# Strassen steps that split their raw blocks first, five raw slots, transfers on ScalarE's queue: one composite edit of a hybrid decoder block

## The chip, the cores and the metric

The kernel runs on one core of a Trainium2 chip. The metric is the device time of one execution in microseconds (us); lower is better. A profiled execution gives the page and the trace from which every duration below is read.

## The reference, cut to what matters

One decoder block on 256 tokens of width 4096, all in float32:

```python
h = rmsnorm(x, norm_w)                       # 256 x 4096
proj = h @ w_in                              # 4096 x 20480
u_p, z_p, u_c, b_c, c_c, z_c, g_logit = split(proj)   # 2048 each, g_logit 8192
y_pool = (pooled_means(u_p) @ pool_w) * pool_scale * silu(z_p)
y_conv = b_c * (conv3(c_c * u_c) + conv_b) * silu(z_c)
br = [y_pool @ w_branch[0], y_conv @ w_branch[1]]     # 2048 x 4096 each
merged = sum(sigmoid(g_logit + gate_b) * br)
out = rmsnorm(x + merged @ w_out, final_norm_w)
```

Nearly all work is in the three products with `w_in`, `w_branch` and `w_out`. Every weight is used once, so all weights stream through the core.

## The kernel before, in words

**Units and steps.** The products are cut into 32 units of 1024 output columns: 20 for `w_in` (names `cz`, `cb`, `cu`, `cc` for the convolution branch, `pz`, `pu` for the pooling branch, `g` for the gates), 8 for `w_branch` (`b`) and 4 for `w_out` (`o`). A unit is a row of steps; a step multiplies 256 tokens by one 256 x 1024 block of weights. A `w_in` or `w_out` unit has 16 steps, a `w_branch` unit 8. Each float32 value is split in two parts, a rounded high part and the rest, and each product is made of three matmuls (high by high, high by low, low by high).

**Two kinds of steps.** A plain step, `P`, is eight block products: 24 matmuls of 128 x 512. A Strassen step, `S`, is seven block products: 21 matmuls, paid for with sums of weight blocks that are formed on the core (and with sums of activations that stand ready in `arena`). The texts such as `NINE` or `TEN` give the order of P and S steps of a unit; `NINE` has nine S, `TEN` ten, `SIX5` six.

**What a step needs.** The weight block of 128 x 2048 is loaded into one of `NRAW = 4` slots of `raw` (`issue_load`, line 993) by SP's queue. For an S step the load is cut in two, and a third, accumulating DMA by POOL's queue adds quarter 2 into quarter 3. Then the block is prepared: ScalarE rounds high parts into cells of `ring` (`highs`, line 245), VectorE subtracts to get low parts (`lows`, line 249). In an S step of before, ScalarE rounds all four quarters, VectorE forms three sums in `parts` (function `added`, line 305), and `split` (line 312) makes high and low parts of the sums. A P step holds 8 cells of the ring of `CELLS = 27`, an S step 14; TensorE's groups free them two by two.

**What sets the order.** The program order of every engine is written out by hand. `pump` (line 1009) issues loads, the next one as soon as the step `NRAW` before it is prepared in program order, and lays preparation as far ahead as the ring has cells. Work after a unit (its epilogue) is a queue of items, one taken for every six matmuls; `gap(n)` is n empty items. `combine` (line 442) evacuates the Strassen corner sums `J` into the result: for late units by two accumulating DMAs by POOL's queue (`gather`). All plain transfers between buffers and DRAM scratch (`move`, line 82: gates, merged rows, stage fills, row parameters) go to SP's queue, in program order among the weight loads. `evacuate` (line 421) copies a finished PSUM bank to `E` or `Y`, and a new unit's first matmul into this bank comes after it.

A unit with ten S steps holds one more activation operand than stands in the arena; it is swapped into `side` by a DMA of POOL's queue (`side_load`, line 544), once in such a unit.

Of the kernel before, what the change touches and what calls it, by code (L numbers as in the profile page):

```python
# [15 lines left out]
P = 128  # L16
T = 256
D = 4096
HALF = D // 2
# [4 lines left out]
KB = 256  # L24

ND, NS, NB = 8, 6, 2
CELLS = 27
NRAW = 4
EARLY = 3
AHEAD = 4  # L30
TICK = 6
# [6 lines left out]
SEVEN3 = "PPPSPSPSPSPSPSPS"  # L38
NINE = "PSPSPSPSSPSPSSPS"
NINE_A = "PSPSSPSPSSPSPSPS"  # L40
NINE_P = "PSPSSPSPSSPSSPSP"
HOST = "PPBPPMMPSSPSSPSSPSS"
TEN = "PSPSSPSSPSSPSSPS"
OUT3 = "PSPSPSPSPSPSSPPP"
# [7 lines left out]
def hybrid_block(ctx: ExitStack, tc: tile.TileContext, x, xc, prm, rows_in, w_in, pool_w, w_branch, w_out, out):  # L52
# [27 lines left out]
        return pin(nc.scalar.dma_start(dst, src))  # L80

    def move(dst, src):
        return pin(nc.sync.dma_start(dst, src))

    def aside(dst, src):
        return pin(nc.gpsimd.dma_start(dst, src))
# [10 lines left out]
    def sb(name, shape, dt=F32):  # L97
        return upper.tile(shape, dt, name=name)
# [8 lines left out]
    J = blocks("J", [P, 4, NH])  # L107
    ident = blocks("ident", [P, P])
    raw = sb("raw", [P, NRAW, 2 * NU])
    parts = sb("parts", [P, 3, NH])  # L110
    sa = sb("sa", [P, 8, P])
    Y = sb("Y", [P, 2, NU])
    par = sb("par", [P, 112])
# [131 lines left out]
    def highs(cells, src):  # L245
        for i, c in runs(cells):
            act(ring[:, c], src[:, i])
# [11 lines left out]
    class Step:  # L259
# [7 lines left out]
        def first(self):  # L267
            if self.kind == "B":
                return []

            def rounded(cells):
                self.q = self.raw.rearrange("p (i c) -> p i c", i=4)
                self.cells = cells
                if self in steps[:2]:
                    for i in range(4):
                        if self is steps[0] and i == 0:
                            copy(ring[:, cells[0]], self.q[:, 0])
                        else:
                            highs(cells[i:i + 1], self.q[:, i:i + 1])
                elif self.halved:  # L280
                    for i in (0, 2):
                        highs(cells[i:i + 2], self.q[:, i:i + 2])
                else:
                    highs(cells, self.q)

            return [(4, None, rounded)]

        def rest(self):
            if self.kind == "P":
                def rests(to):  # L290
                    self.lows = to
                    if self in steps[:2]:
                        for i in range(4):
                            if self is steps[0] and i % 2 == 0:
                                x_low(0, 1 - i // 2)
                            lows(to[i:i + 1], self.cells[i:i + 1], self.q[:, i:i + 1])
                    elif self.halved:
                        for i in (0, 2):
                            lows(to[i:i + 2], self.cells[i:i + 2], self.q[:, i:i + 2])
                    else:  # L300
                        lows(to, self.cells, self.q)

                return [(4, None, rests)] + self.mid
            if self.kind == "S":
                def added(to):
                    q, d = self.q, self.cells
                    self.lows = to
                    sub(parts[:, 0], q[:, 3], q[:, 1])
                    lows(to[3:4], d[3:4], q[:, 3:4])
                    sub(parts[:, 1:3], q[:, 0:3:2], parts[:, 0:1].to_broadcast([P, 2, NH]))  # L310

                def split(cells):
                    self.sum_cells, self.sum_lows = cells[0:3], cells[3:6]
                    highs(cells[0:1], parts[:, 0:1])
                    highs(cells[1:3], parts[:, 1:3])
                    lows(self.lows[0:3], self.cells[0:3], self.q[:, 0:3])
                    lows(cells[3:6], cells[0:3], parts)

                return [(4, None, added)] + self.mid + [(6, None, split)]
            if self.kind == "B":  # L320
                def base(cells):
                    self.cells, self.lows = cells[0:4], cells[4:8]
                    highs(self.cells, quarters(E))
                    lows(self.lows, self.cells, quarters(E))

                return [(8, lambda: self.unit.flags.get("base"), base)]

            def pooled(cells):
                self.pool_cells, self.pool_lows = cells[0:2], cells[2:4]
                q = quarters(E)[:, 2 * self.g:2 * self.g + 2]  # L330
                highs(self.pool_cells, q)
                lows(self.pool_lows, self.pool_cells, q)

            def rests(to):
                self.lows = to
                lows(to, self.cells, self.q)

            return [(4, None, rests), (4, lambda: self.unit.flags.get(f"pooled{self.g}"), pooled)]
# [2 lines left out]
            return cell(self.cells[i]), cell(self.lows[i]), [self.cells[i], self.lows[i]]  # L341

        def formed(self, i):
            return cell(self.sum_cells[i]), cell(self.sum_lows[i]), [self.sum_cells[i], self.sum_lows[i]]

        def groups(self):
            gs = []
# [18 lines left out]
            else:  # L366
# [1 line left out]
                prods = {"M1": (A11, plain(2), ("F", 0, 0)),  # L368
                         "N3": (Q3, plain(1), ("E", 0, 0)),
                         "M2": (A12, plain(0), ("E", 0, 1)),  # L370
                         "N5": (Q5, plain(3), ("F", 0, 1)),
                         "N6": (Q6, formed(0), ("F", 1, 1)),
                         "N4": (A22, formed(1), ("E", 1, 1)),
                         "N7": (Q7, formed(2), ("F", 1, 0))}
# [67 lines left out]
    def combine(u):  # L442
        d = u.dst
        if u.s:
            corner_sums(u)
            assert u.cornered
            q = J.rearrange("p (n t) c -> p t n c", n=2)
            d4 = d.rearrange("p t (n c) -> p t n c", n=2)
            if u.late:
                for t, n in ((0, 4), (1, 2)):  # L450
                    queue.extend(gap(n) + [lambda t=t: gather(d4[:, t], q[:, t])])
            elif u.scaled:
                for t in range(2):
                    stt(d4[:, t], q[:, t], rin[:, t:t + 1], d4[:, t], ALU.mult, ALU.add)
            else:
                add(d4, d4, q)
        u.flags["base"] = True
        hush[0] = now[0] + (HUSH if u.late else 0)
        quiet[0] = now[0] + QUIET
        if u.urgent:  # L460
            u.urgent()
# [96 lines left out]
    def silu_y(late):  # L558
        def silu(t):
            act(Y[:, t], Y[:, t], AF.Silu, **(dict(scale=rin[:, t:t + 1]) if late else {}))  # L560
        return gap(12 if late else 3) + [lambda: silu(0), None, lambda: silu(1)]

    def rescale(d):
        return gap(12) + [lambda: act(d[:, 0], d[:, 0], scale=rin[:, 0:1]), None,
                          lambda: act(d[:, 1], d[:, 1], scale=rin[:, 1:2])]

    def conv_units(c, first):
        base = 2 * HALF + c * NU

        def b_epi(u):  # L570
            def product(t):
                stt(E[:, t], E[:, t], rin[:, t:t + 1], Y[:, t], ALU.mult, ALU.mult)
            return gap(12) + [lambda: product(0), None, lambda: product(1)] + gap(5) + [lambda: move(g_d[c], E)]

        def c_epi(u):
            def inner(j):
# [16 lines left out]
                        kb = 8 * c + b  # L593
                        stt(y[:, b, s:], v[:, i, 0:T - s], tap_col(2 - s, kb), y[:, b, s:], ALU.mult, ALU.add)

            items = [lambda: move(Y, g_d[c])] + gap(6) + pairs(transposes(E, inner)) + gap(5) + pairs(transposes(Y, outer))
            for j, n in enumerate((1, 7, 8, 8)):
                items += gap(n) + [lambda j=j: taps(j)]
            return items + [None, lambda: mul(chan(E), chan(J), chan(Y))] + gap(5) + [lambda: put(y_d[1, c], chan(E))]

        u = in_unit(f"cz{c}", base + 3 * HALF, lambda u: silu_y(u.late) + (gap(4) + side_items(ND - 1) + side_items(ND - 2) if first else []),
                    FIRST if first else SIX5, dst=Y)
        u.late = not first
        in_unit(f"cb{c}", base + HALF, b_epi, TEN if c else NINE_A).late = True
        u = in_unit(f"cu{c}", base, lambda u: rescale(Y), NINE, dst=Y)
        u.late = True
        in_unit(f"cc{c}", base + 2 * HALF, c_epi, NINE_A).urgent = lambda: mul(E, E, Y)

    def pool_units(c):
        u = in_unit(f"pz{c}", HALF + c * NU, lambda u: silu_y(True) + gap(4) + band_items(c), HOST if c else SIX5, dst=Y)  # L610
        u.late = True
        in_unit(f"pu{c}", c * NU, lambda u: [], NINE_P).urgent = lambda: None

    def band_items(c):
        if c == 0:
# [114 lines left out]
    def branch_unit(n, c):  # L730
        def epi(u):
# [16 lines left out]
            def stored():  # L748
                put(m_d[c], chan(turned))
                merged[c] = now[0] + STORED  # L750
            return gap(2) + [gated, None, lambda: add(E, E, Y), None,
                lambda: c < 3 and move(Y, gates_d[0, c + 1])] + gap(4) + pairs(transposes(E, copy)) + gap(4) + [stored]

        text = (B1 if c else B1_FIRST) if n else B0_MORE if c else B0
        u = Unit(f"b{n}_{c}", lambda i: w_branch[n, c, i], seq_y(text), y_ops[n], epi)
# [7 lines left out]
    def out_unit(c):  # L763
# [5 lines left out]
        def epi(u):  # L769
            def row(t):  # L770
                gather(E[:, t], xrows[:, t, cs])

            def square(t):
                act(Y[:, 1], E[:, t], AF.Square, accum_out=ossq[:, t, c:c + 1])
            return gap(8) + [lambda: row(0), None, None, lambda: row(1)] + gap(12) + [start] + gap(6) + [
                lambda: square(0), lambda: square(1),
                lambda: mul(E, E, Y[:, 0:1].to_broadcast([P, 2, NU]))] + gap(5) + [lambda: move(o_d[c], E)]

# [341 lines left out]
    for u in units:  # L1120
# [28 lines left out]
        for st in u.steps:  # L1149
            assert st.prepared, (u.name, st.kind)  # L1150
            run_step(u, st)
            if u.text is TEN and st.kind == "S" and st.op in x_ops[:ND] and st is not u.steps[-1]:
                side_load(2 * ND - 3 - x_ops.index(st.op))
            state["now"] += 1
            if state["now"] == OPENED:
# [114 lines left out]
```

## Time and profile before

| what | value |
|---|---|
| median of 3 runs | 2411.51 us (2397.87 to 2412.62) |
| the profiled execution | 2411.59 us |
| its span, first to last instruction | 2409.9 us |
| TensorE (PE) busy | 2356.2 us, 98% |
| VectorE (DVE) busy | 2085.2 us, 87% |
| ScalarE (ACT) busy | 1499.1 us, 62% |
| mean HBM rate | 251 GB/s |

Times in the profile are counted from the first instruction. PE is TensorE's matmuls, PEld its weight loads, DVE is VectorE, ACT ScalarE, POOL GpSimd, SP SyncE. Consecutive matmuls overlap in the records, so a busy PE is not one at its peak; how many matmuls start in a stretch says more. A wait is shown with the engine, tile and line that ended it.

### The profile page before, as it was taken

The page shows a single profiled execution, that of the slowest core. Times are in us where ns is not written, and L with a number is a line of the kernel's source. Part 1 is how long each engine was busy: PE and PEld are TensorE (multiplying, and loading weights), DVE is VectorE, ACT ScalarE, POOL GpSimd, SP SyncE. Part 2 cuts the span into 40 slices and gives each one's busy share as a digit, 9 for nine tenths or more (in the row PEclk, how much of TensorE's full clock was granted, in tenths as well). Part 3 has the DMA queues.
Part 4 walks back from the last instruction along what each step waited for, and adds up shares of the span by engine and source line. Part 5 has one row for each costly group of instructions (what it writes and reads, how often), then busy time and mean ns, then how long its engine had stood idle before and what let it go on. Part 6 is the DMA issues. An engine that isn't in the chain of part 4 may idle for free.

```text
span 2409.9 us, 28848 instructions
## 1 busy us (share of the span) xinstructions
PE 2356.2 (98%) x10424; PEld 1938.3 (80%) x10424; DVE 2085.2 (87%) x2034; ACT 1499.1 (62%) x1590; POOL 284.8 (12%) x342
## 2 busy tenths in 40 slices
PE   9999999999999999999999999999999999999996
PEld 7888888888888788788787787778888888887875
DVE  8789888998889879879898898888898889898967
ACT  6665656666666556656666666666666656566654
POOL 0011100110101101101111111111000000011110
PEclk9999999999999999999999999999999999999998
DMA  9789876988868768768998899899878788888986
GB/s 369 233 262 273 242 261 204 280 264 247 262 224 243 236 206 246 249 207 247 282 276 265 257 294 270 254 301 270 285 243 288 254 279 287 258 239 276 289 261 237
DMA packets 167712, 627.71 MB, mean 260 GB/s; under 512 B 17424, under 2 KB 25872, under 8 KB 135568
## 3 DMA queue, kind: packets, MB, share of 16 engines
q1 hardware_dynamic: 118864, 526.04, 61.1%
q0 software_dynamic: 48128, 98.59, 23.1%
q8 instruction: 81, 1.33, 0.2%
q10 hardware_dynamic: 576, 1.24, 0.1%
q14 instruction: 63, 0.52, 0.1%
HBM read 579.66 MB, written 25.17 MB: 251 GB/s over the span
## 4 chain that ended last, share of the span: by engine, by line
PE 73%; DMA 14%; DVE 8%; issue 3%; ACT 2%; POOL 0%; SPq 0%; DVEq 0%; ACTq 0%; POOLq 0%
PE sums L1048 54%; PE shared L1048 17%; DMA raw<-in_w_in_dram 9%; DVE ring L62 5%; DMA gates_d<-E 2%; DMA raw<-in_w_out_dram 2%; DVE parts L62 2%; ACT ring L59 1%; PE shared L693 1%; DMA E<-J 1%; PE shared L479 1%; DMA Y<-in_rows_dram 1%; DMA o_d<-E 0%; ACT E L59 0%; DVE J L62 0%
## 5 line engine op out<-in xcount | busy, mean ns | idle before, releaser
L1048 PE MATMUL sums<-ring,arena 128*128 128x512 f32 x7011 | 1653.3, 391 | 37.4 <-DVE ring L62 22.2
L1048 PEld LDWEIGHTS sums<-ring,arena 128*128 128x128 f32 x7011 | 1314.7, 188 | 324.7 <-DVE ring L62 31.8
L62 DVE TENSOR_TENSOR ring<-raw,ring 128x512 fp32r<-128x512 f32 (+3 forms) x904 | 1085.6, 1220 | 148.2 <-ACT ring L59 77.5
L59 ACT ACTIVATE ring<-raw 128x1024 fp32r<-128x1024 f32 (+3 forms) x661 | 882.8, 1370 | 323.7 <-DMA raw<-in_w_in_dram 101.3
L59 ACT ACTIVATE ring<-parts 128x1024 fp32r<-128x1024 f32 (+1 forms) x451 | 372.6, 840 | 384.8 <-DVE parts L62 290.1
L1048 PE MATMUL shared<-ring,arena 128*128 128x512 f32 x2241 | 542.0, 389 | 0.1
L1048 PEld LDWEIGHTS shared<-ring,arena 128*128 128x128 f32 x2241 | 421.0, 188 | 88.4 <-DVE ring L62 0.5
L62 DVE TENSOR_TENSOR ring<-parts,ring 128x1536 fp32r<-128x1536 f32 (+2 forms) x258 | 391.6, 1529 | 29.8 <-ACT ring L59 19.5
L89 POOL DMA_DIRECT2D raw<-in_w_in_dram x168 | 145.4, 866 | 1408.3 <-DMA raw<-in_w_in_dram 559.5
L62 DVE TENSOR_TENSOR parts<-raw,parts 128x1024 f32<-128x1024 f32 x222 | 270.6, 1219 | 0.0
L62 DVE TENSOR_TENSOR parts<-raw 128x512 f32<-128x512 f32 x222 | 152.4, 687 | 37.9 <-issue 31.1
L62 DVE TENSOR_TENSOR J<-J 128x512 f32<-128x512 f32 (+1 forms) x90 | 78.3, 870 | 39.3 <-ACT J L59 36.8
L1048 PE MATMUL sums<-ring,last_pair 128*128 128x512 f32 x306 | 77.1, 390 | 3.6 <-DVE ring L62 3.6
L59 ACT ACTIVATE E<-sums 128x512 f32<-128x512 f32 x76 | 42.0, 598 | 54.9 <-DMA gates_d<-E 25.9
L59 ACT ACTIVATE J<-shared 128x512 f32<-128x512 f32 x128 | 68.7, 626 | 11.7 <-PE shared L479 10.7
L1048 PEld LDWEIGHTS sums<-ring,last_pair 128*128 128x128 f32 x306 | 57.2, 188 | 16.6 <-DVE ring L62 4.9
L89 POOL DMA_DIRECT2D raw<-in_w_out_dram x31 | 27.1, 873 | 287.1 <-DMA raw<-in_w_out_dram 180.9
L89 POOL DMA_DIRECT2D raw<-in_w_branch_dram x23 | 20.0, 869 | 298.3 <-DMA raw<-in_w_branch_dram 174.3
L1048 PE MATMUL shared<-ring,last_pair 128*128 128x512 f32 x216 | 51.9, 389 | 0.0
L1048 PE MATMUL shared<-ring,side 128*128 128x512 f32 x207 | 50.7, 389 | 0.0
L1048 PEld LDWEIGHTS shared<-ring,last_pair 128*128 128x128 f32 x216 | 40.5, 188 | 8.5
L1048 PEld LDWEIGHTS shared<-ring,side 128*128 128x128 f32 x207 | 38.9, 188 | 8.1
(124 smaller groups left out, 674.5 us busy)
## 6 DMA issues: line engine op xcount, KB each, us to landing
raw<-in_w_in_dram SPq DMA_DIRECT2D x150, 1024.0 KB, 7.0
raw<-in_w_in_dram SPq DMA_DIRECT2D x168, 768.0 KB, 6.4
raw<-in_w_in_dram SPq DMA_DIRECT2D x176, 256.0 KB, 5.5
raw<-in_w_in_dram POOLq DMA_DIRECT2D x168, 256.0 KB, 6.7
raw<-in_w_branch_dram SPq DMA_DIRECT2D x41, 1024.0 KB, 7.4
raw<-in_w_out_dram SPq DMA_DIRECT2D x33, 1024.0 KB, 7.2
raw<-in_w_out_dram SPq DMA_DIRECT2D x31, 768.0 KB, 6.8
raw<-in_w_branch_dram SPq DMA_DIRECT2D x23, 768.0 KB, 6.3
```

Of the source, the lines that this page charges most:

```text
L59: return pin(nc.scalar.activation(dst, src, func, **kw))
L62: return pin(nc.vector.tensor_tensor(out=dst, in0=a, in1=b, op=op))
L89: return pin(nc.gpsimd.dma_start(dst, src, accum_op=ALU.add))
L479: pin(nc.tensor.transpose(shared(j)[:, i * T + t * P:i * T + (t + 1) * P], src[:, t, c:c + P], ident))
L693: pin(nc.tensor.matmul(o, a, b, start=(k, i) == (0, 0), stop=(k, i) == (3, 2)))
L1048: pin(nc.tensor.matmul(ps, lhs, rhs, start=n == 0, stop=n == u.total[b] - 1))
```

## The change

An S step keeps the same sums, written to other places. ScalarE first rounds the three plain quarters that are used as they are (0, 1, 2) and VectorE makes their low parts (`whole`). Then VectorE writes the sums over the raw block itself (quarter 1 becomes quarter 3 minus quarter 1, then quarters 0 and 2 have it subtracted), and the four formed quarters are split in two pairs (`outer`, `inner`). `parts` is gone, `raw` has five slots, the ring 26 cells. `move` goes to ScalarE's queue. `cz1`, `cu0`, `cu1`, `cc0`, `cc1`, `pz0`, `pu0`, `pu1` have one S step in place of a P step each. Gaps in several epilogues are shifted by one to six items.

```diff
-CELLS = 27
-NRAW = 4
+CELLS = 26
+NRAW = 5
...
-NINE_P = "PSPSSPSPSSPSSPSP"
+TEN_P = "PSPSSPSSPSSPSSSP"
+SEVEN5 = "PPPPPSPSPSSPSPSS"
...
     def move(dst, src):
-        return pin(nc.sync.dma_start(dst, src))
+        return pin(nc.scalar.dma_start(dst, src))
...
-    parts = sb("parts", [P, 3, NH])
...
-                    highs(cells, self.q)
-            return [(4, None, rounded)]
+                    highs(cells, self.q[:, 0:len(cells)])
+            return [(3 if self.kind == "S" else 4, None, rounded)]
...
-                def added(to):
-                    q, d = self.q, self.cells
+                def whole(to):
                     self.lows = to
-                    sub(parts[:, 0], q[:, 3], q[:, 1])
-                    lows(to[3:4], d[3:4], q[:, 3:4])
-                    sub(parts[:, 1:3], q[:, 0:3:2], parts[:, 0:1].to_broadcast([P, 2, NH]))
-                def split(cells):
-                    self.sum_cells, self.sum_lows = cells[0:3], cells[3:6]
-                    highs(cells[0:1], parts[:, 0:1])
-                    highs(cells[1:3], parts[:, 1:3])
-                    lows(self.lows[0:3], self.cells[0:3], self.q[:, 0:3])
-                    lows(cells[3:6], cells[0:3], parts)
-                return [(4, None, added)] + self.mid + [(6, None, split)]
+                    lows(to, self.cells, self.q[:, 0:3])
+                def outer(cells):
+                    q = self.q
+                    self.outer = cells
+                    sub(q[:, 1], q[:, 3], q[:, 1])
+                    sub(q[:, 0:3:2], q[:, 0:3:2], q[:, 1:2].to_broadcast([P, 2, NH]))
+                    highs(cells[0:2], q[:, 1:4:2])
+                    lows(cells[2:4], cells[0:2], q[:, 1:4:2])
+                def inner(cells):
+                    q = self.q
+                    self.inner = cells
+                    highs(cells[0:2], q[:, 0:3:2])
+                    lows(cells[2:4], cells[0:2], q[:, 0:3:2])
+                return [(3, None, whole)] + self.mid + [(4, None, outer), (4, None, inner)]
...
-                         "N5": (Q5, plain(3), ("F", 0, 1)),
+                         "N5": (Q5, formed(3), ("F", 0, 1)),
...
             if u.late:
-                for t, n in ((0, 4), (1, 2)):
+                for t, n in ((0, 2), (1, 1)):
                     queue.extend(gap(n) + [lambda t=t: gather(d4[:, t], q[:, t])])
...
-        return gap(12 if late else 3) + [lambda: silu(0), None, lambda: silu(1)]
+        return gap(15 if late else 3) + [lambda: silu(0), None, lambda: silu(1)]
     def rescale(d):
-        return gap(12) + [lambda: act(d[:, 0], d[:, 0], scale=rin[:, 0:1]), None,
+        return gap(14) + [lambda: act(d[:, 0], d[:, 0], scale=rin[:, 0:1]), None,
...
-                    FIRST if first else SIX5, dst=Y)
+                    FIRST if first else SEVEN5, dst=Y)
...
-        u = in_unit(f"cu{c}", base, lambda u: rescale(Y), NINE, dst=Y)
+        u = in_unit(f"cu{c}", base, lambda u: rescale(Y), TEN, dst=Y)
...
-        in_unit(f"cc{c}", base + 2 * HALF, c_epi, NINE_A).urgent = lambda: mul(E, E, Y)
+        in_unit(f"cc{c}", base + 2 * HALF, c_epi, TEN).urgent = lambda: mul(E, E, Y)
...
-        u = in_unit(f"pz{c}", HALF + c * NU, lambda u: silu_y(True) + gap(4) + band_items(c), HOST if c else SIX5, dst=Y)
+        u = in_unit(f"pz{c}", HALF + c * NU, lambda u: silu_y(True) + gap(4) + band_items(c), HOST if c else SEVEN5, dst=Y)
...
-        in_unit(f"pu{c}", c * NU, lambda u: [], NINE_P).urgent = lambda: None
+        in_unit(f"pu{c}", c * NU, lambda u: [], TEN_P).urgent = lambda: None
...
-            return gap(8) + [lambda: row(0), None, None, lambda: row(1)] + gap(12) + [start] + gap(6) + [
+            return gap(6) + [lambda: row(0), None, lambda: row(1)] + gap(12) + [start] + gap(8) + [
...
-            if u.text is TEN and st.kind == "S" and st.op in x_ops[:ND] and st is not u.steps[-1]:
+            if u.text in (TEN, TEN_P) and st is next(q for q in u.main if q.kind == "S"):
                 side_load(2 * ND - 3 - x_ops.index(st.op))
```

More of the change, by code (lines that the diff above doesn't have):

```diff
@@ L343, in formed @@
         def formed(self, i):
-            return cell(self.sum_cells[i]), cell(self.sum_lows[i]), [self.sum_cells[i], self.sum_lows[i]]
+            c, j = ((self.outer, 0), (self.inner, 0), (self.inner, 1), (self.outer, 1))[i]
+            return cell(c[j]), cell(c[2 + j]), [c[j], c[2 + j]]
         def groups(self):
@@ L572, in product @@
                 stt(E[:, t], E[:, t], rin[:, t:t + 1], Y[:, t], ALU.mult, ALU.mult)
-            return gap(12) + [lambda: product(0), None, lambda: product(1)] + gap(5) + [lambda: move(g_d[c], E)]
+            return gap(15) + [lambda: product(0), None, lambda: product(1)] + gap(5) + [lambda: move(g_d[c], E)]
         def c_epi(u):
@@ L594, in taps @@
                         stt(y[:, b, s:], v[:, i, 0:T - s], tap_col(2 - s, kb), y[:, b, s:], ALU.mult, ALU.add)
-            items = [lambda: move(Y, g_d[c])] + gap(6) + pairs(transposes(E, inner)) + gap(5) + pairs(transposes(Y, outer))
+            items = gap(2) + [lambda: move(Y, g_d[c])] + gap(6) + pairs(transposes(E, inner)) + gap(5) + pairs(transposes(Y, outer))
             for j, n in enumerate((1, 7, 8, 8)):
@@ L751, in epi @@
             return gap(2) + [gated, None, lambda: add(E, E, Y), None,
-                lambda: c < 3 and move(Y, gates_d[0, c + 1])] + gap(4) + pairs(transposes(E, copy)) + gap(4) + [stored]
+                ] + gap(4) + pairs(transposes(E, copy)) + [
+                    lambda: c < 3 and move(Y, gates_d[0, c + 1])] + gap(4) + [stored]
         text = (B1 if c else B1_FIRST) if n else B0_MORE if c else B0
```

## The prediction

> **What bounds the kernel now.** I read the page's engine sums first, then its chain, then the waits, then single units.
>
> ```profile
> span 2409.9 us, 28848 instructions
> PE 2356.2 (98%) x10424; PEld 1938.3 (80%) x10424; DVE 2085.2 (87%) x2034; ACT 1499.1 (62%) x1590; POOL 284.8 (12%) x342
> PE 73%; DMA 14%; DVE 8%; issue 3%; ACT 2%; POOL 0%; SPq 0%; DVEq 0%; ACTq 0%; POOLq 0%
> ```
>
> TensorE sets the time: 98% busy, 73% of the chain. But 14% of the chain is DMA, so in places it is a transfer that TensorE in the end waits for. How fast can it go? In the timeline of an undisturbed stretch:
>
> ```profile
> 526.38 7.64 PE L1048 MATMUL sums<-ring,arena 128*128 128x512 f32 x33
> 533.86 2.88 PE L1048 MATMUL shared<-ring,arena 128*128 128x512 f32 x12
> ```
>
> 33 matmuls start in 533.86 - 526.38 = 7.48 us, so one takes 0.2267 us. A unit with nine S and seven P steps is 9 x 21 + 7 x 24 = 357 matmuls, 80.9 us; one with ten S is 354, 80.3 us. Now the stretches of single units, cut where their first matmul starts: `cu1` and `cc1` (nine S), `cb1` (ten S), the six gate units with ten S, `pu1` and `pu0` (nine S). A row has the stretch, its length, the busy us of PE, PEld, DVE, ACT and POOL with their instructions, the granted clock, the DMA engines' busy share and GB/s.
>
> ```profile
> 506.50:587.60 81.10, 81.10 (x359) 66.97 (x358) 72.94 (x68) 49.44 (x52) 10.31 (x11) 1.00 0.88 258
> 587.60:668.90 81.30, 81.30 (x359) 66.89 (x358) 70.27 (x65) 51.31 (x54) 8.60 (x9) 1.00 0.83 252
> 425.00:506.50 81.50, 80.78 (x355) 66.30 (x355) 73.97 (x69) 52.62 (x53) 12.54 (x14) 1.00 0.91 272
> 1120.70:1626.30 505.60, 489.54 (x2125) 399.46 (x2123) 442.81 (x410) 326.94 (x333) 79.97 (x89) 0.99 0.92 273
> 939.70:1022.60 82.90, 81.14 (x358) 66.90 (x357) 74.78 (x78) 52.04 (x54) 15.36 (x21) 1.00 0.79 244
> 755.50:841.60 86.10, 82.32 (x359) 66.61 (x358) 74.64 (x75) 52.12 (x52) 17.70 (x38) 1.00 0.80 247
> ```
>
> The convolution units run at their floor (81.1 and 81.3 against 80.9). A gate unit takes 505.6 / 6 = 84.3 us against 80.3: **in this kernel ten S steps cost more than nine, though they hold fewer matmuls.** What they wait for is in the waits of TensorE, and of ScalarE and VectorE ahead of it:
>
> ```profile
> PE sums L1048 <- DVE ring L62: 25.8, 17, 9.3
> PE sums L1048 <- ACT E L59: 13.5, 7, 2.6
> ACT E L59 <- DMA gates_d<-E: 25.9, 5, 5.8
> ACT ring L59 <- DMA raw<-in_w_in_dram: 101.3, 57, 6.7
> SPq L77 <- DVE ring L62: 1875.6, 544, 12.2
> ```
>
> The columns are total us, times, longest. Two waits hold nearly all that TensorE loses: prepared weights (25.8) and the evacuation of `E` at a unit's end (13.5).
>
> **Why prepared weights are late.** The last row says that SP nearly always stands before a load whose slot VectorE has not yet read out. The chain, asked for 1286 to 1350 us alone, is a row of such loads:
>
> ```profile
> by line: DMA raw<-in_w_in_dram 78.5%; DVE ring L62 13.8%; issue 8.5%; ACT ring L59 3.0%; ACT J L59 2.5%; ACT E L59 2.4%; DVE J L62 2.3%; DVEq L62 0.2%; POOLq L89 0.2%; ACTq L59 0.1%
> 1302.27 7.33 DMA raw<-in_w_in_dram
> ...
> raw<-in_w_in_dram SPq DMA_DIRECT2D x150, 1024.0 KB, 7.0
> ...
> raw<-in_w_in_dram SPq DMA_DIRECT2D x176, 256.0 KB, 5.5
> raw<-in_w_in_dram POOLq DMA_DIRECT2D x168, 256.0 KB, 6.7
> L59 ACT ACTIVATE ring<-raw 128x2048 fp32r<-128x2048 f32 x254 | 486.5, 1917 | 280.0 <-DMA raw<-in_w_in_dram 94.8 <-PE sums L1048 86.8 <-issue 45.5
> ```
>
> The last column of a transfer is the median from issue to landing. An S load is two transfers in a row, 5.5 + 6.7 = 12.2 us. A slot is then in use for some 6 us (1.92 of rounding, then 0.69 + 1.22 + 1.75 of subtraction by rows quoted below). That is 18 us of a cycle of four slots, 4 x 5.0 = 20 us, before any queueing: no slack. A P slot needs 7.0 and 1.92 + 2.29. So where S steps are dense the load latency is the bound.
>
> **Why the evacuation is late.** `gates_d<-E` must have read `E` before the next unit writes it. In the timelines of ScalarE and SP:
>
> ```profile
> 1350.06 1.05 ACT L59 ACTIVATE E<-E 128x1024 f32<-128x1024 f32 x1
> ...
> 1353.77 4.27 SPq L77 DMA_DIRECT2D raw<-in_w_in_dram  x2
> 1358.15 0.37 SPq L83 DMA_DIRECT2D gates_d<-E  x1
> ...
> 1369.45 0.60 ACT L59 ACTIVATE E<-sums 128x512 f32<-128x512 f32 x1 [4.60 <-DMA gates_d<-E]
> ...
> 1372.38 4.10 PE L1048 MATMUL sums<-ring,arena 128*128 128x512 f32 x11 [2.42 <-ACT E L59]
> ```
>
> The sigmoid ends at 1351.1, the store is issued at 1358.15 behind two loads and lands 11 us later; ScalarE has waited 4.60 us, TensorE 2.42. So about 2.2 us of lateness are free. What follows the stall costs too:
>
> ```profile
> 1374.00:1377.50 3.50, 3.50 (x10) 2.74 (x9) 2.14 (x3) 3.50 (x7) 0.40 (x1) 0.52 0.62 107
> ```
>
> At a granted clock of 0.52 ten matmuls start where 15 should: 1.2 us. The Trainium skill's page "TensorE: Matmul & The Clock Gate" (What's actually happening) has the clock fall after about 3.4 us without matmuls; by that rule a 2.42 us stall would leave it alone and this term be nothing. The row shows the drop, and the row decides.
>
> **The change, part by part.**
>
> *Matmuls.* Eight P steps become S: 8 x 3 = 24 matmuls less, 24 x 0.2267 = **-5.4 us**.
>
> *VectorE and ScalarE in an S step.* From the groups by shape:
>
> ```profile
> L62 DVE TENSOR_TENSOR ring<-raw,ring 128x1536 fp32r<-128x1536 f32 x200 | 350.4, 1752 | 2.3 <-PE sums L1048 1.9 <-ACT ring L59 0.4
> L62 DVE TENSOR_TENSOR ring<-raw,ring 128x1024 fp32r<-128x1024 f32 x351 | 417.8, 1220 | 17.2 <-PE sums L1048 12.3 <-ACT ring L59 4.2 <-issue 0.3
> L62 DVE TENSOR_TENSOR parts<-raw 128x512 f32<-128x512 f32 x222 | 152.4, 687 | 37.9 <-issue 31.1 <-DVE ring L62 3.0 <-DMA raw<-in_w_out_dram 1.7
> L62 DVE TENSOR_TENSOR parts<-raw,parts 128x1024 f32<-128x1024 f32 x222 | 270.6, 1219 | 0.0
> L62 DVE TENSOR_TENSOR ring<-raw,ring 128x2048 fp32r<-128x2048 f32 x51 | 116.3, 2287 | 25.2 <-ACT ring L59 12.4 <-PE shared L1048 7.2 <-PE sums L1048 2.2
> ```
>
> Before: two of 512 columns, one of 1024 into `parts`, two of 1536, so 2 x 687 + 1219 + 2 x 1752 = 6.10 us; after: 1752 + 687 + 1219 + 2 x 1220 = 6.10. ScalarE rounds 3584 columns either way. So a step costs the same; an S instead of a P costs VectorE 6.1 - 2.29 = 3.8, or 3.45 where neighbours overlap by 0.08 us each. That makes 72.94 + 3.45 = 76.4 of 80.3 us in `cu1`, 73.7 in `cc1`, 78.2 in `pu1`: 95, 92 and 97%. Up to such a fill it is hidden; these six units have little cover left. I bound its cost by 0 and by rival C's 27.5 and take **+3**, near the nearest row, `cb1`, which lost 0.7 at 74.0.
>
> *Five slots.* The cycle grows to 25 us. The slot is held one subtraction longer (lows of the inner pair, last instead of `parts`), 1.7 us, so 3.3 us of slack are won. Of the 25.8 us of waits 9.3 lie in `o3` (below) and some 2 at the start (1.8 of the waits up to 338 us), before the fifth slot counts. Of the other 14.5 I take **-11**; bounds 0 and -14.5.
>
> *Ring.* One cell less, finer blocks (3, 3, 4, 4 for 4, 4, 6). Preparation can start as soon as three cells are free; one cell less is a fourteenth of an S step, 0.35 us of lead. I take 0; bounds -1 and +3.
>
> *Transfers on ScalarE's queue.* SP's stores no longer stand behind slot waits, and the gate store is one item (six matmuls, 1.4 us) earlier by the shifted gaps. The wait before `E` shrinks from 4.6 by this 1.4, by the wait behind loads, and by what the store spends in one ring with 1 MB loads; 2.4 us are enough. I take **-12.5** of 13.5, and **-3.5** for three clock drops (1.2 each, after three such stalls). In `o3`:
>
> ```profile
> 2322.49 19.62 SPq L77 DMA_DIRECT2D raw<-in_w_out_dram  x8
> 2342.15 0.48 SPq L83 DMA_DIRECT2D Y<-in_rows_dram  x1
> ...
> 2354.63 2.29 DVE L62 TENSOR_TENSOR E<-E,Y 128x2048 f32<-128x2048 f32 x1 [13.44 <-DMA Y<-in_rows_dram]
> 2340.88 0.86 POOL L89 DMA_DIRECT2D E<-in_x_dram  x1 [7.15 <-DMA E<-J]
> ...
> E<-in_x_dram POOLq DMA_DIRECT2D x6, 512.0 KB, 12.7
> ```
>
> The row parameters were issued after 19.62 us of waiting loads; VectorE stood 13.44 us, TensorE 9.3. On ScalarE's queue they come in time. But the last rows of x are added by POOL only from 2340.88, and such a transfer lands after 12.7 us by the median, so VectorE would be held till about 2353 all the same; that chain starts four to six items (5 to 8 us) earlier. I take **-7**; bounds 0 and -9.3.
>
> What it adds: a `move` now holds ScalarE till its data is there, and behind it stand the roundings that VectorE waits for. SP's own waits at these places bound it:
>
> ```profile
> SPq L83 <- DVE arena L62: 32.5, 15, 3.8
> SPq L83 <- DVE E L62: 24.9, 5, 7.9
> ```
>
> With some 75 issues of about 0.4 us, as the two above (0.37 and 0.48), 30 us, that is 87 us of ScalarE, which has 38% idle. Between 0 and 44 (half, as TensorE paid 13.5 of 25.9 above) I take **+2**, near 0, because ScalarE reaches the place later than an idle SP.
>
> *Six more side loads* (0.5 MB each by POOL) land long before the last S step that needs them: 0.
>
> Sum: -5.4 + 3 - 11 - 12.5 - 3.5 - 7 + 2 = -34.4. The profiled execution took 2411.6 (span 2409.9 and 1.7 around it), as the median of 2411.5: **2377 us**.
>
> **The rivals.**
>
> *A, everything goes and nothing new comes:* -5.4 - 14.5 - 13.5 - 3.5 - 9.3 = -46: 2365. Against it: `pu0`'s loss comes with POOL's 17.7 us of other work, which stays.
>
> *B, the new queue buys nothing.* In the gate units the 16 DMA engines are 92% busy; if the store lands no sooner whoever issues it, the boundary, the clock and `o3` stay: -5.4 + 3 - 11 + 2 = -11.4: 2400. The Trainium skill's "DMA: Bandwidth & Descriptors" (Issuing engines are not separate DMA queues) says just this: all issuers share the same DMA engines, and another one saves only issue time. Against B stands that the store and the row parameters lost time before issue, behind waiting loads.
>
> *C, VectorE becomes the bound: slower than before.* In the gate units it is filled to 442.81 / 505.6 = 87.6%. If this is its own limit and not the loads', five slots bring nothing there, and the six units run at VectorE's time over 0.876: `cu` 87.2 (+6.1 each), `cc` 73.7 / 0.876 = 84.1 (+2.9), `pu` 89.3 (+3.2 and +6.4), together +27.5; with -23 of the queue and -1.4 for `cz1` and `pz0` it is +3: 2415. It decides wherever the reachable fill is under the 92 to 97% that these units need. Against it: `cb1` reached 91% and lost little, and the chain in the gate units is loads, not VectorE.
>
> *D, ScalarE is held by the transfers:* +33 to +87 in place of +2: 2408 to 2462.
>
> **How the numbers follow.** Forecast (2366 to 2388) 0.52, A 0.10, B 0.14, C 0.15, D 0.09. A measurement of this kernel tells about 1%, 24 us, from no change. Under 2387.4 lie A, nearly all of the forecast and the better edge of B: 0.65. Over 2435.6 lies D's upper half: 0.05. Within 1%: 0.30. The range for 8 in 10 leaves out A's best and the far ends of C and D: 2360 to 2406.
>
> **What would show it.** In the profile after: `ACT E <- DMA gates_d<-E` gone or under 10 us, PEclk 1.00 in the gate units; gate units at 81 to 82 us; ScalarE's waits on raw loads well under 101 us; `DVE E <- DMA Y<-in_rows_dram` gone; `cu`, `cc` at 80 to 82, `pu` 83 to 85. Wrong if VectorE's share of the convolution units stays under 90% while they grow past 83 us (C), or if new waits of ScalarE before its DMA issues reach tens of us (D).

## The result and the profile after

The changed kernel takes 2398.64 us (2394.99 to 2404.57, 20 runs) against 2408.38 us of before (2397.87 to 2419.74, 20 runs): ratio 0.9957, 95% interval 0.9947 to 0.9968. It is faster, by some 10 us (0.4%) where 34 were forecast. The profiled execution took 2402.2 us, its span 2400.5. The page after:

```profile
span 2400.5 us, 28579 instructions
PE 2353.2 (98%) x10400; PEld 1937.4 (81%) x10400; DVE 2167.9 (90%) x2009; ACT 1500.1 (62%) x1572; POOL 295.1 (12%) x356
```

VectorE is busy 83 us longer, ScalarE as long as before. TensorE's waits after:

```profile
PE sums L1054 <- DVE ring L63: 13.0, 13, 3.3
PE sums L1054 <- ACT E L60: 6.2, 2, 5.9
PE sums L1054 <- ACT ring L60: 5.1, 3, 1.9
...
PE sums L1054 <- ACT arena L60: 2.3, 1, 2.3
```

Prepared weights and the evacuation fell from 25.8 and 13.5 to 13.0 and 6.2, and new names came: ScalarE's roundings into `ring` and `arena`. Where, the stretches tell. After: `cz1`, `cu1`, `pz0`, the six gate units, `g1_0`, `b0_0`, `o0` (columns as in the prediction):

```profile
337.00:428.50 91.50, 88.83 (x397) 72.29 (x396) 79.70 (x77) 53.88 (x62) 8.61 (x10) 0.98 0.73 223
508.70:589.00 80.30, 80.30 (x356) 66.48 (x356) 78.45 (x69) 50.18 (x50) 11.71 (x13) 1.00 0.91 271
669.20:760.70 91.50, 87.76 (x397) 71.07 (x396) 77.66 (x73) 53.03 (x60) 7.75 (x9) 1.00 0.73 222
1121.70:1603.20 481.50, 481.50 (x2126) 398.80 (x2126) 457.51 (x397) 327.83 (x330) 79.24 (x88) 1.00 0.95 285
1603.20:1692.20 89.00, 84.67 (x364) 69.17 (x363) 71.59 (x70) 52.93 (x56) 10.37 (x11) 0.98 0.88 271
1692.20:1740.50 48.30, 42.39 (x188) 34.77 (x186) 38.09 (x41) 30.21 (x33) 4.31 (x5) 0.98 0.85 260
2046.00:2136.50 90.50, 87.31 (x384) 71.28 (x383) 79.99 (x86) 52.86 (x56) 6.96 (x8) 0.98 0.78 239
```

The same units before, without `cu1` and the gates, which stand in the prediction:

```profile
338.40:425.00 86.60, 86.60 (x399) 72.03 (x399) 74.37 (x74) 52.80 (x62) 6.03 (x7) 1.00 0.72 225
668.90:755.50 86.60, 86.60 (x400) 72.03 (x399) 74.25 (x75) 52.70 (x61) 6.04 (x7) 1.00 0.73 225
1626.30:1710.40 84.10, 84.05 (x364) 69.23 (x365) 71.32 (x74) 55.18 (x60) 9.51 (x10) 0.98 0.94 286
1710.40:1753.60 43.20, 42.31 (x187) 34.72 (x185) 38.79 (x42) 30.58 (x34) 4.37 (x5) 1.00 0.85 266
2050.50:2136.40 85.90, 84.98 (x383) 70.24 (x382) 77.04 (x86) 51.48 (x56) 6.95 (x8) 1.00 0.83 255
```

The gate units stand at 481.5 / 6 = 80.25 us, the floor of their 354 matmuls, at clock 1.00; before they took 505.6. The whole balance, each unit from its first matmul to the next unit's:

| units | change, us |
|---|---|
| six gate units with ten S | -24.1 |
| `o1`, `o2`, `o3` | -12.3 |
| `cu`, `cc`, `cb1` | -4.7 |
| `pu0`, `pu1` | -4.4 |
| `cz0` | -0.9 |
| `cz1`, `pz0` | +9.8 |
| `g1_0`, `b0_0`, `b1_0` | +13.6 |
| the other `b` units | +5.1 |
| `o0` | +4.5 |
| before the first and after the last matmul, rest | +4.0 |

So 46 us were won, more than the 39 forecast, and 37 were lost again, where 5 were forecast. The experiments ask about both halves.

### The profile page after: what moved, and what is told of

It is laid out like the page before. It is cut to its first block, busy times and chain, and to the rows that moved or that the text cites. A ratio compares the mean times of both kernels' runs of the same rounds, so it can differ in the third digit from the quotient of the medians.

```text
span 2400.5 us, 28579 instructions
## 1 busy us (share of the span) xinstructions
PE 2353.2 (98%) x10400; PEld 1937.4 (81%) x10400; DVE 2167.9 (90%) x2009; ACT 1500.1 (62%) x1572; POOL 295.1 (12%) x356
## 5 line engine op out<-in xcount | busy, mean ns | idle before, releaser
L60 ACT ACTIVATE ring<-raw 128x1024 fp32r<-128x1024 f32 (+3 forms) x1096 | 1237.8, 1175 | 769.8 <-DVE raw L63 528.9
L1054 PE MATMUL sums<-ring,arena 128*128 128x512 f32 x6873 | 1621.0, 391 | 26.7 <-DVE ring L63 10.5
L63 DVE TENSOR_TENSOR ring<-raw,ring 128x1024 fp32r<-128x1024 f32 (+3 forms) x1123 | 1464.4, 1343 | 114.9 <-ACT ring L60 65.3
L1054 PEld LDWEIGHTS sums<-ring,arena 128*128 128x128 f32 x6873 | 1289.7, 188 | 304.2 <-DVE ring L63 18.1
L1054 PE MATMUL shared<-ring,arena 128*128 128x512 f32 x2283 | 557.9, 392 | 0.3 <-DVE ring L63 0.2
L63 DVE TENSOR_TENSOR raw<-raw 128x512 f32<-128x512 f32 x460 | 440.7, 958 | 17.0 <-DMA raw<-in_w_out_dram 2.2
L63 DVE TENSOR_TENSOR J<-J 128x512 f32<-128x512 f32 (+1 forms) x90 | 78.2, 869 | 16.7 <-ACT J L60 14.6
L1054 PE MATMUL shared<-ring,side 128*128 128x512 f32 x261 | 64.5, 390 | 1.5 <-DVE ring L63 1.5
L1054 PEld LDWEIGHTS shared<-ring,side 128*128 128x128 f32 x261 | 48.8, 188 | 12.5 <-DVE ring L63 2.1
L90 POOL DMA_DIRECT2D raw<-in_w_branch_dram x23 | 19.9, 867 | 313.4 <-DMA raw<-in_w_branch_dram 132.1
L90 POOL DMA_DIRECT2D E<-J x28 | 39.1, 1475 | 11.5 <-ACT ring L60 11.5
L63 DVE TENSOR_TENSOR E<-E,Y 128x2048 f32<-128x2048 f32 x9 | 20.6, 2289 | 11.3 <-ACT Y L60 11.3
L75 DVE SCALAR_TENSOR_TENSOR Y<-E,par,Y 128x255 f32<-128x255 f32 (+1 forms) x32 | 13.8, 479 | 12.7 <-ACT Y L60 12.7
```

The lines of the kernel that those rows point to most:

```text
L60: return pin(nc.scalar.activation(dst, src, func, **kw))
L63: return pin(nc.vector.tensor_tensor(out=dst, in0=a, in1=b, op=op))
L75: return pin(nc.vector.scalar_tensor_tensor(out=dst, in0=a, scalar=s, in1=b, op0=op0, op1=op1, **kw))
L90: return pin(nc.gpsimd.dma_start(dst, src, accum_op=ALU.add))
L1054: pin(nc.tensor.matmul(ps, lhs, rhs, start=n == 0, stop=n == u.total[b] - 1))
```

## The experiments

**Stage fills back on SP's queue.**

```diff
 def fetch(self, st):
-    move(st[:, 4:8]..., self.src)
+    load(st[:, 4:8]..., self.src)
```

> The changed kernel with the 28 or so stage fills (y_d and m_d blocks into sa, sb, sc) on SP's queue again; all other transfers stay on ScalarE's. Theory 1 (ScalarE is held at a fill until VectorE has read the stage out, and the roundings behind it come late): g1_0, b0_0, b1_0, b1_3 and o0, which grew by 5.0, 5.0, 3.6, 3.2 and 4.5 us over before, give back most of these 21 us: about 2380 us. Theory 2 (the new order of the S step itself is slower there, whatever the queue): no change, 2398.

Measured 2386.43 us, ratio 0.9894 (0.9865 to 0.9923). Its `g1_0`, `b0_0` and `o0`:

```profile
1602.70:1685.00 82.30, 82.30 (x365) 68.17 (x364) 71.68 (x70) 52.80 (x57) 10.36 (x11) 1.00 0.95 296
1685.00:1727.10 42.10, 42.10 (x187) 34.88 (x186) 38.49 (x41) 30.74 (x34) 4.36 (x5) 1.00 0.93 273
2034.80:2122.30 87.50, 85.39 (x383) 70.20 (x383) 78.34 (x84) 52.05 (x54) 6.96 (x8) 1.00 0.81 244
```

`g1_0` and `b0_0` return to their floors, `o0` gets back 3.0 of 4.5 us, `b1_0` 1.9 of 3.6 and `b1_3` 0.3 of 3.2; `b1_1` loses 5.9, which is why the whole gains 12 and not 18. The mechanism stands in the changed kernel's trace, in the timelines of ScalarE, VectorE and TensorE in `g1_0`:

```profile
1683.43 1.09 DVE L63 TENSOR_TENSOR arena<-sb,arena 128x896 fp32r<-128x896 f32 x1
1686.06 2.36 DVE L63 TENSOR_TENSOR ring<-raw,ring 128x1024 fp32r<-128x1024 f32 x2 [1.54 <-ACT ring L60]
...
1684.60 0.33 ACTq L84 DMA_DIRECT2D sb<-y_d  x1
1684.97 2.95 ACT L60 ACTIVATE ring<-raw 128x1024 fp32r<-128x1024 f32 x3 [2.71 <-DVE arena L63]
...
1686.08 0.49 PE L1054 MATMUL sums<-ring,arena 128*128 128x512 f32 x1 [1.57 <-ACT ring L60]
```

A fill may be fetched when VectorE has read the stage, at 1684.5. ScalarE reaches the fetch early and stands 2.71 us, the rounding behind it starts at 1684.97, VectorE then waits 1.54 us for it and TensorE 1.57. With the fills on SP, SP stood 37.8 us in 15 waits of this kind (`SPq L78 <- DVE arena L63`); only loads stood behind them, and `g1_0` and `b0_0` ran at their floors.

**Six S steps again in `cz1` and `pz0`.**

```diff
-                    FIRST if first else SEVEN5, dst=Y)
+                    FIRST if first else SIX5, dst=Y)
...
-        u = in_unit(f"pz{c}", ..., HOST if c else SEVEN5, dst=Y)
+        u = in_unit(f"pz{c}", ..., HOST if c else SIX5, dst=Y)
```

> The changed kernel with six S steps again in cz1 and pz0 (6 matmuls, 1.4 us, more for TensorE). Theory A (in these two units VectorE is over-full in the stretch of S steps, with the convolution's taps in it; each grew by 4.9 us): both return to 86.6 us, 2389. Rival B (ScalarE's transfers of y_d delay it there, or the new S order): they stay at 91 or grow by 0.7 each, 2398 to 2400.

Measured 2392.69 us, 0.9925 (0.9901 to 0.9948). `cz1` and `pz0`:

```profile
338.30:425.40 87.10, 86.95 (x400) 71.99 (x399) 75.53 (x72) 52.16 (x60) 6.88 (x8) 1.00 0.73 221
666.10:753.10 87.00, 86.85 (x399) 71.92 (x398) 75.57 (x72) 52.13 (x60) 6.90 (x8) 1.00 0.74 225
```

4.4 us return in each, so one S step more cost 4.4 where it holds three matmuls less. The whole gained 6 us, not the 9 expected: `cz0` (+2.3) and `b1_1` (+1.8), above all, took the rest.

**Both edits together.**

> Both edits: fills on SP's queue and six S steps in cz1 and pz0. If the two losses are apart, the gains add: 2398 - 18 - 9 = about 2371 us. If both are one cause (ScalarE late), less than the larger one is added: 2378 or more.

Measured 2374.86 us, 0.9853 (0.9829 to 0.9876): 24 us less than the change, where the edits gave 12 and 6 one at a time. So the two losses are apart, and without them the kernel is 2 us from the 2377 forecast for the whole change. In part that is luck, for the terms of that sum came out otherwise, as the next runs show.

**All transfers on SP's queue**, the rest of the change kept.

```diff
 def move(dst, src):
-    return pin(nc.scalar.dma_start(dst, src))
+    return pin(nc.sync.dma_start(dst, src))
```

> The changed kernel with every transfer on SP's queue as before; five slots, the new S order and the eight S steps stay. If the new queue took the waits at the ends of the gate units away, these come back: waits of ScalarE for gates_d over 20 us, about +15 us there, and the fills' 18 us go: 2395. If the five slots or the shorter gaps took them away, only the fills' loss goes: 2380.

Measured 2385.20 us, 0.9897 (0.9873 to 0.9922): 13 us better than the change with its queue. The six gate units:

```profile
1122.10:1608.80 486.70, 483.25 (x2126) 398.28 (x2125) 456.78 (x397) 326.45 (x328) 79.21 (x88) 1.00 0.94 280
```

81.1 us each: new step, slots and shifted gaps give 18.9 of the 24.1 us without the queue, the queue the last 5.2. That lies between the two cases that I had set apart. `o3` takes 88.0 us in this run and 87.8 in the changed kernel, so what it gained there did not need the queue either.

**One part at a time on the kernel before.** First the new S step alone, four slots (the diff's `whole`, `outer`, `inner` and three first cells; `parts` gone, nothing else).

> The kernel before with the new S step alone (plain quarters first, sums over the raw block, four formed quarters); four slots, 27 cells, SP's queue, old texts and gaps. Theory 1 (load latency in a cycle of four slots is the gate units' bound): a slot is held longer, so the gate units stay at 83 to 86 us or grow: 2405 to 2420. Rival (the early low parts of the plain quarters, ready for the first products, were what the gate units lacked): they fall to 81 to 82 us, about 2392.

Measured 2411.51 us, 1.0012 (0.9997 to 1.0027), no change, and the gate units stayed at 84.7 us each. Both are what I had named for the theory of the slots. But below the time everything moved. The gate units, ScalarE's waits on raw loads, then TensorE's waits:

```profile
1114.10:1622.40 508.30, 490.34 (x2126) 401.61 (x2125) 456.61 (x410) 325.37 (x334) 79.95 (x89) 0.99 0.91 270
...
ACT ring L59 <- DMA raw<-in_w_in_dram: 3.1, 5, 1.5
ACT ring L59 <- DMA raw<-in_w_branch_dram: 0.7, 2, 0.5
...
PE sums L1052 <- ACT E L59: 20.2, 6, 4.6
PE sums L1052 <- DVE ring L62: 8.1, 2, 6.5
```

The waits on loads fell from 101 to 3 us with four slots still, and TensorE's waits for weights from 25.8 to 8.1, of which one of 6.5 (in `o3`). The evacuation rose from 13.5 to 20.2, and the mean granted clock of the profiled run fell from 0.994 to 0.991; the two took back what was won. My theory of the slots falls as a mechanism, though its number came: for the loads, four would have served in this order.

Then five slots and 26 cells added.

> The same with five slots and 26 cells. Theory 1: the gate units fall to 80.5 to 81.5 us except for waits on gates_d at their ends (2 us each), pu0 and o2 lose their stalls: about 2385. Rival (the slots are not the bound): no better than the new order alone.

Measured 2399.44 us, 0.9960 (0.9944 to 0.9976): 12 us less, not the 26 expected; the gate units took 492.9 us together. TensorE's waits for weights and for the evacuation:

```profile
PE sums L1052 <- DVE ring L62: 14.7, 4, 10.2
PE sums L1052 <- ACT E L59: 8.4, 6, 2.1
```

For weights one wait of 10.2, in `o3`, is most of the sum. For the evacuation 20.2 fell to 8.4, and the traces show by what step. In the five gate units whose store holds up the next unit, the store of the gates landed 78.9 to 80.6 us after the unit's start, with four slots 81.6 to 84.1; the next unit began 2.6 to 3.0 us after the landing, in both. On the mean the sigmoid ended earlier (62.2 us after the unit's start against 64.7) and the transfer took less from issue to landing (9.2 us against 10.4). Why a fifth slot shortens these two is open.

**The queue alone** on the kernel before.

> The kernel before with the transfers on ScalarE's queue, nothing else. If the queue takes away the waits at the ends of the gate units as I forecast: -12 there, -3 of clock, up to -9 in o3; against it the stage fills hold ScalarE as measured in the changed kernel, +12 in the branch units and g1_0: about 2400. If the queue buys nothing in the gate units: 2420.

Measured 2393.57 us, 0.9930 (0.9909 to 0.9952), the largest gain of a single part. The gate units and `b0_0`, and below them TensorE's waits:

```profile
1125.80:1613.60 487.80, 484.14 (x2126) 397.90 (x2125) 443.65 (x410) 329.48 (x337) 79.96 (x89) 1.00 0.95 283
1696.90:1743.70 46.80, 42.91 (x187) 34.54 (x186) 39.65 (x43) 31.45 (x36) 4.37 (x5) 1.00 0.86 261
```

```profile
PE sums L1048 <- DVE ring L62: 25.2, 18, 5.5
PE sums L1048 <- ACT E L59: 2.4, 1, 2.4
```

The evacuation's waits fall from 13.5 to 2.4 us as forecast, the gate units by 17.8 us; prepared weights stay where they were; `b0_0` shows the price of the fills.

**The queue but for the fills.**

> The kernel before with the transfers on ScalarE's queue except the stage fills. If fills alone hold ScalarE: b0_0 and b1_0, which grew by 3.5 and 2.0 us with the whole queue moved, fall back to 42 to 43 and 41.6; cz1 and pz0 (no fills there) stay at 88.6; about 2388. If any transfer holds it there: 2393.

Measured 2392.99 us, 0.9931 (0.9906 to 0.9956). `b0_0` and `b1_0` came back to 43.1 and 41.7 us, but `pu0`, `pu1` and `o3` lost 6.0 together, so the whole stayed. The units behave as for the first case, the whole as for the second. `cz1` and `pz0` stood at 88.6 as expected, 2.0 us over the kernel before. What moved the `pu` units is open.

**The eight S steps alone** on the kernel before.

> The kernel before with the eight S steps alone (texts and the place of the side load). If S steps beyond nine are paid for by load latency: cu and cc grow by 1 to 4 us each as the gate units did, pu by some 2, cz1 and pz0 by some 4: 2420 to 2430. If four slots suffice for them: 2411 - 5 = 2406.

Measured 2417.45 us, 1.0032 (1.0018 to 1.0045): slower, though less than I expected. `cz1`, `pz0` and `cb1`:

```profile
337.40:423.50 86.10, 86.10 (x397) 71.41 (x396) 76.38 (x77) 54.01 (x62) 6.88 (x8) 1.00 0.72 225
672.60:758.80 86.20, 86.20 (x396) 71.37 (x396) 75.90 (x76) 54.03 (x62) 6.90 (x8) 1.00 0.74 235
423.50:506.50 83.00, 81.69 (x356) 66.13 (x355) 75.24 (x70) 53.07 (x54) 12.54 (x14) 1.00 0.90 270
```

`cb1` and `cu1` grew by 1.5 and 4.0 us, but `cz1` and `pz0` gain 0.5 each: with the old step seven S fit there. The loss of these two needs the new step.

**New step and the eight, four slots, SP's queue.**

> The new S step and the eight S steps on the kernel before, four slots, SP's queue, old gaps. Theory (a new S step takes VectorE 6.3 us from one to the next instead of 5.8, since its in-place sums wait for each other, and this over-fills cz1 and pz0): both at 90 to 92 us, against 86.0 and 86.2 with the eight alone; about 2414. Rival (the over-fill comes from the slots, the ring of 26 or the gaps): both stay at 86 to 87, about 2405.

Measured 2429.08 us, 1.0090 (1.0061 to 1.0118). `cz1` took 89.6 and `pz0` 93.0 us: neither slots, queue nor gaps are needed for that loss. The whole is 15 us over what I had expected; the gate units took 512.9 us together and `cb1` 85.5, and why is open. A reason for the loss of `cz1` is in VectorE's timeline. An S step behind another, first in the kernel with the eight alone, then in the changed one:

```profile
414.33 0.69 DVE L63 TENSOR_TENSOR parts<-raw 128x512 f32<-128x512 f32 x1
414.93 0.69 DVE L63 TENSOR_TENSOR ring<-raw,ring 128x512 fp32r<-128x512 f32 x1
415.54 1.22 DVE L63 TENSOR_TENSOR parts<-raw,parts 128x1024 f32<-128x1024 f32 x1
416.67 1.75 DVE L63 TENSOR_TENSOR ring<-raw,ring 128x1536 fp32r<-128x1536 f32 x1
418.34 1.75 DVE L63 TENSOR_TENSOR ring<-parts,ring 128x1536 fp32r<-128x1536 f32 x1
```

```profile
412.88 1.94 DVE L63 TENSOR_TENSOR raw<-raw 128x512 f32<-128x512 f32 x2
414.83 2.43 DVE L63 TENSOR_TENSOR ring<-raw,ring 128x1024 fp32r<-128x1024 f32 x2
417.42 1.76 DVE L63 TENSOR_TENSOR ring<-raw,ring 128x1536 fp32r<-128x1536 f32 x1 [0.15 <-ACT ring L60]
419.21 1.95 DVE L63 TENSOR_TENSOR raw<-raw 128x512 f32<-128x512 f32 x2
```

Old, the five instructions end at 420.09 after 5.76 us. Where the next S step follows at once, the kernel before shows the whole period:

```profile
1427.97 0.68 DVE L62 TENSOR_TENSOR parts<-raw 128x512 f32<-128x512 f32 x1
...
1431.98 1.75 DVE L62 TENSOR_TENSOR ring<-parts,ring 128x1536 fp32r<-128x1536 f32 x1
1433.77 0.69 DVE L62 TENSOR_TENSOR parts<-raw 128x512 f32<-128x512 f32 x1
```

That is 5.80 us from start to start. New, the step's sums start at 412.88 and the next step's at 419.21: 6.33 us. The first two sums, the second of which reads the first, take 1.95 from start to the next start (414.83 - 412.88); with another instruction between them they took 2.34 - 0.61 = 1.73. The low parts before the sums take 1.79 instead of 1.67, for the first sum writes over what they read, and the next step's first low parts wait for ScalarE. In `cz1` the last eleven steps hold seven S, four P, sixteen tap instructions of 0.44 and one product of 2.2: 7 x 6.33 + 4 x 2.3 + 7.0 + 2.2 = 63 us of VectorE beside 55.1 us of matmuls (243 x 0.2267). At 5.80 a step it is 59, and that did not show: `cz1` took 86.1 with the eight alone and 91.5 in the changed kernel. That steps prepared ahead cover 4 us and not 8 is argued, not measured. Nor was VectorE busy throughout. Before the taps it stood for ScalarE, in `cz1` with the eight alone, then in the changed kernel:

```profile
DVE Y L75 <- ACT Y L60: 2.0, 3, 1.6
```

```profile
DVE Y L75 <- ACT Y L60: 6.0, 3, 3.7
```

How the 5.4 us divide between the longer period and these waits is open.

**The change without the eight.**

> The changed kernel with the eight S steps undone (nine in cu, cc, pu, six in cz1, pz0); order, slots, queue and gaps stay. From the units of the changed kernel: cu and cc lose their 0.7 to 1.0 us each (+3.5 in all), pu gains or loses under 1 each, cz1 and pz0 win 4.5 each: 2398 - 9 + 3.5 = about 2393, so the eight together cost 5 us as they stand. If the eight are worth their matmuls: 2404.

Measured 2391.61 us, 0.9929 (0.9905 to 0.9953): as they stand the eight cost about 7 us. `pu0` and `pu1` stood at 80.9, their floor, against 83.0 and 81.6 with ten S.

**The accumulating DMA awaited again**, on the new step alone:

```diff
+                if self.kind == "S":
+                    act(first_look, self.q[:, 3, 0:1])
...
                     highs(cells, self.q[:, 0:len(cells)])
```

> The new S step alone on the kernel before (2411.5 us), with one added instruction of ScalarE in each S step, on one column: it reads the last quarter, the one that the accumulating DMA completes, ahead of the first rounding, and its result is not used. Theory 1 (the new step gains because its first rounding and low parts need not wait for the accumulating DMA): ScalarE's waits on raw loads go from 3 back to 80 us or more, TensorE's waits for prepared weights from 8 to over 20, 2425 to 2440 us. Rival (the gain is that the low parts of the plain quarters are made first): waits stay under 20 us and only the 222 instructions of some 0.2 us on an engine with 38% idle are added, 2411 to 2417.

Measured 2448.74 us, 1.0178 (1.0153 to 1.0202), 37 us more than without. The added instruction in the groups by shape:

```profile
L59 ACT ACTIVATE first_look<-raw 128x1 f32<-128x1 f32 x222 | 43.0, 194 | 111.7 <-DMA raw<-in_w_in_dram 54.5 <-DMA raw<-in_w_branch_dram 34.5 <-DMA raw<-in_w_out_dram 22.2
```

It waits 111.7 us for loads, and the time went past the 2425 to 2440 that I had expected. TensorE's waits for weights rose less than I had named: into `sums` 10.3 us, into `sums` and `shared` 19.9, against 8.1 and 10.6 without the look; the evacuation's rose from 20.2 to 25.8. This shows what the new step lives by: its first rounding needs only the plain quarters, and the second DMA of the load runs beside it. With that taken away it is 37 us slower than the old step, which has the same wait (101.3 us), so the new step costs something elsewhere that this gain covers. How much of the 37 us is the added instruction itself, 43.0 us of ScalarE, was not measured.

**All that was found, together:** fills on SP, six S in `cz1` and `pz0`, nine in `pu`; ten only in `cu`, `cc` and `cb1`.

> The changed kernel with the stage fills on SP's queue, six S steps in cz1 and pz0 and nine in pu0 and pu1; ten stay in cu and cc. In the run without the eight, pu0 and pu1 stood at 80.9 us, their floor, against 82.2 and 81.5 with ten and both other edits: 2374.9 - 1.9 = about 2373 us. If the stall only moves on to the next units: 2375 or more.

Measured 2372.42 us, 0.9853 (0.9830 to 0.9876), a version that beats both kernels, but within the noise of the run with both edits (2374.86). `pu0` and `pu1` stand at 80.9; `o0` and `o3` are longer than in that run, by 1.4 and 1.1 us.

## Why the prediction was right or wrong

The direction held and the time lies in the range, but the time was off by 22 us and the change by 25 (10 where 34 were forecast). Two terms made it.

- **"It costs the same" (VectorE in an S step) failed.** The durations are equal, 6.10 us, but I had the overlap of neighbours in the trace (0.08 us each) and did not ask whether it survives when one instruction reads what the last one wrote, or writes over what it read. The period is 6.33 instead of 5.80. And I priced only `cu`, `cc` and `pu`, at +3, and named no cost for `cz1` and `pz0`, whose S steps stand in the last eleven of sixteen. Cost: 9.8 us there. That this loss needs the new step and the seventh S step is shown (86.1 and 86.2 without the first, 87.1 without the second); that the longer period makes all of it is not. The convolution units that I feared went to their floor at 97.7% fill (78.45 of 80.3), so rival C's limit of 87.6% was no limit of VectorE.
- **"+2" for ScalarE's queue failed; it was rival D's mechanism, at the fills**, though smaller than D's +33. About 23 us went in `g1_0`, the `b` units and `o0`; with the fills on SP 12 us of the whole returned. I argued that ScalarE comes to the place later than an idle SP. It does not, where the fetch is laid directly behind VectorE's last read of the stage. The bound that I had worked out (0 to 44) held the value; the choice near its lower end was wrong.
- **-11 for five slots: the size came, by luck, and the cause was another.** TensorE's waits for weights fell without the slots, by the step's order. I had read the sum 5.5 + 6.7 us of an S load and missed that the diff takes its second part out of the way of the first rounding. The slots then gave 12 us, but in the evacuation's waits. The chain of loads in the gate units was real; a longer cycle was not its only cure.
- **-12.5, -3.5 and -7 for the queue held in part:** alone it took the evacuation's waits to 2.4 us and 4.9 us from `o3`; in the changed kernel the clock drops are gone from the gate units (1.00). But the terms were not additive: step, slots and gaps alone bring the gates to 81.1, and the queue had 5.2 left to win there. They also bring `o3` to 88.0, so the 7.5 us that it gained, near my 7, were not the queue's there; the shifted gaps are the likely cause, since new step and slots with the old gaps left it at 96.0. Rival B, the new queue buying nothing, falls as a mechanism, though its 2400 us came out.
- **-5.4 for 24 matmuls:** -0.7 to -1.0 in each of `cu` and `cc`; `cz1` and `pz0` gave back more than that.

## What to carry to other kernels

Ask of every wait that a change moves to another engine what stands behind it there: the same wait for a stage cost `g1_0` and `b0_0` nothing on the load queue, and in front of roundings the whole kernel 12 us. Take the fill of a helping engine over the stretch in which the work must be done, not over the unit, and take an instruction's cost from the distance between starts in a like chain. Where an input comes by two transfers, begin with what the first one brings.

## What the hardware showed that I had not expected

A VectorE instruction mostly starts some 0.08 us before its neighbour's recorded end (414.93 against 414.33 + 0.69 in the lines of the old step). One that depends on its neighbour does not. The second sum reads the first one's result, and the two, of 0.69 and 1.22 us, take 1.95. The first sum writes over what the low parts before it read, and starts 0.03 after their end (419.21 against 417.42 + 1.76). The old step has one such place, where `parts` is written over (1433.77 against 1431.98 + 1.75). In the new step the low parts behind the sums start late too (414.83 against 412.88 + 1.94); why is open. VectorE is busy 83 us longer in all. The eight steps alone give 27 of it (2112.5 us against 2085.2), the new step alone 56 (2141.3): 0.25 us for each of 222 S steps, about three lost overlaps.

The gate transfers landed sooner on ScalarE's queue. Of all transfers of `gates_d`, in the run with every transfer on SP's queue and the rest of the change kept, then in the changed kernel:

```profile
DMA to landing us min/median/max: 7.6/10.0/12.9
```

```profile
DMA to landing us min/median/max: 4.4/6.6/10.6
```

These are times from issue to landing, and rival B had the store land no sooner whoever issues it. With the queue alone the gain is smaller, from a median of 9.1 to 8.5 us. Why they land sooner is open, and so are the 2.9 us more after the last matmul, and why `b1_1` takes 41.5 to 47.8 us from one variant to the next.
